# RWKV-7 in a two-layer hybrid block: a unit's two pairs prepared beside each other, and 32x32 triangles inverted as 16x16 blocks in the second layer

## The chip, the cores and the metric

One core of one Trainium2 chip. The metric is the time of one execution in device microseconds. Of the kernel before there are three: 2938.81, 2939.93 and 2939.21 us, median 2939.21 us.

## What is computed

A block of a latent diffusion generator, two layers deep, width 1024, in f32: 256 context tokens and 256 latent tokens, batch 1. Each layer normalizes and modulates the tokens, projects them with one wide matrix, and runs three mixers beside each other, each in both directions: mLSTM (4 heads), a depthwise convolution with an RG-LRU, and RWKV-7 (16 heads of 64). Sigmoid gates merge the three; an output projection, a residual and a SwiGLU follow. The last layer needs no context output. The mixer of this case is RWKV-7; the state of each head is 64x64, and a token does this:

```python
def step(s, x_t):
    r_t, w_t, k_t, v_t, kap_t, kapa_t = x_t
    s_kap = jnp.einsum('bhvk,bhk->bhv', s, kap_t)
    s = s * w_t[:, :, None, :] - s_kap[..., None] * kapa_t[:, :, None, :] + v_t[..., None] * k_t[:, :, None, :]
    return s, jnp.einsum('bhvk,bhk->bhv', s, r_t)
```

The kernel does it in chunks of 32 tokens. For each chunk, head and direction it needs the inverse of a unit triangular 32x32 matrix, built from products of `kap` and the keys.

## The kernel before

A layer is written in four parts. The first weaves the RWKV-7 work with the projections; the second runs the mLSTM heads and the RG-LRU, with the merge gates' projections beside them; the third merges and projects; the fourth is the SwiGLU. The weight blocks are f32, split by ScalarE (`whi`) and VectorE (`wlo`) into two parts, so that a block is 24 matmuls of 128x128 by up to 512 columns.

**Units.** RWKV-7 is done in eight units a layer: four groups of four heads (two pairs of two heads), each for 256 context tokens and then 256 latent tokens. A unit has 16 chunk-directions (8 chunks, 2 directions).
- `rw_load` reads the unit's r, k and v back from DRAM, once the rows of the unit before are done.
- `rw_prep` makes the decays and the rows, first for pair 0, then for pair 1 (`decay`, `rows`), and then the chunks' triangles (`chunks`, line 765): matmuls, a mask on VectorE into the tile `Am` (line 779), and four DMAs that write the strict triangles to DRAM, one matrix a partition row (line 786). Units are prepared one after the other.
- `rw_solve` (line 948) loads the 64 matrices of 32x32 as `N`, one on each of 64 partitions (line 955), inverts them on GpSimd with 30 pairs of a product and a subtraction (lines 961, 963), stores them (line 968) and loads them back into `Am` with four DMAs (line 973). All these go through SyncE's queue, which is in order.
- `rw_tok` transposes values and keys; `rw_chain` (line 977) walks the eight chunks, each needing the state that the one before left: matmuls into `xy`, `u` and `sc`, copies on VectorE and ScalarE between (lines 1032, 1059, 1062, 1079).
- `rw_tail` normalizes and gates the unit's output.

**Order.** `weave` decides at build time in which order the instructions of all these tasks and of the projections (`products`, the fill, last in the list) stand on each engine. It keeps a clock with costs given in the code; a task can yield a wait for a time, for another task's event, or for a lock on PSUM. The fill goes in when nothing else is ready, or first whenever less than `COLS[l]` columns of matmuls lie in the last `TICK` of its clock:

```python
light = [x for x in ready if x[3]]
if light:
    i = light[0]
elif fill in ready:

    if sum(c for _, c in recent) < cols + (HYS if burst else -HYS):
        i = fill
```

On the chip each engine runs its list in order. The gates' projections (`gemm`, line 423; loads on SyncE's queue, line 397; stores, line 1287) are not woven: the framework's scheduler places them after the projections, beside whatever follows. In layer 1 they and part of the projections have 256 columns, as only latent tokens are needed.

Of the kernel before, what the change touches and what calls it, by code (L numbers as in the profile page):

```python
# [11 lines left out]
F32 = mybir.dt.float32  # L12
F32R = mybir.dt.float32r
AF = mybir.ActivationFunctionType
ALU = mybir.AluOpType
# [19 lines left out]
COLS = [3000, 3000]  # L35
GDP = 1
ORD = [0, 0]
SL = 1000
# [61 lines left out]
def constants():  # L100
    c = {}
    c["ident"] = np.eye(128, dtype=np.float32)
    bo = np.zeros((128, 2), np.float32)
    bo[:64, 0] = 1
    bo[64:, 1] = 1
    c["bones"] = bo
    s = np.arange(32)[:, None]
    t = np.arange(32)[None, :]
    mk = np.zeros((2, 64, 64), np.float32)
    for d in range(2):  # L110
        st = (s < t).astype(np.float32)
        inc = ((s <= t) if d == 0 else (s <= 31 - t)).astype(np.float32)
        mk[d, :32, :32] = st
        mk[d, 32:, :32] = st
        mk[d, :32, 32:] = inc
        mk[d, 32:, 32:] = inc
    c["masks"] = np.concatenate([np.concatenate([mk[0], mk[0]], 0), np.concatenate([mk[1], mk[1]], 0)], 1)
    sm = np.ones((128, S), np.float32)
    sm[:, ::CH] = 0
    c["scanm"] = sm  # L120
    return c


CST = [("ident", 128), ("bones", 2), ("masks", 128), ("scanm", S)]
# [87 lines left out]
class KB:  # L212
# [349 lines left out]
    def rw_low(self, l, pss):  # L562
# [4 lines left out]
        for i, n in enumerate(("dd", "ad")):  # L567
            x, xd = (re.tile([128, T], F32, name=t, tag=t) for t in (("kap", "th"), ("bp", "ah"))[i])
# [91 lines left out]
    def rw_prep(self, l, u, ctx_out):  # L660
# [15 lines left out]
        Am = rl.tile([128, 2, 2, 8, 64], F32, name="Am", bufs=3)  # L676
# [22 lines left out]
        def wtanh(j, zw):  # L699
            p = 2 * q + j  # L700
            th = re.tile([128, 2, S], F32, name="th")
            for d in range(2):
                SC.activation(out=th[:, d], in_=zw[:, d], func=AF.Tanh, scale=0.5, bias=self.hdec[:, 8 * d + p:8 * d + p + 1])
                yield self.at("S", 470)
            return th

        def decay(j, th, za):
            p = 2 * q + j
            at = re.tile([128, 2, S], F32, name="at")
# [10 lines left out]
            pp = re.tile([128, 2, 8, 33], F32, name="pp")  # L720
# [7 lines left out]
            kt = re.tile([128, 2, S], F32, name="kt")  # L728
# [36 lines left out]
        def chunks(bks):  # L765


            for d in range(2):
# [14 lines left out]
            for j in range(2):  # L783
                for x in range(2):
                    b = 64 * x + 32 - 32 * j
                    nc.sync.dma_start(out=sc1[x, j].rearrange("q s t -> s q t"), in_=Am[b:b + 32, j, :, :, 0:32].rearrange("p d c t -> p (d c) t"))
# [6 lines left out]
        w = yield from axsplit(w)  # L793
        yield ("lock", "sm")
# [26 lines left out]
        sc1 = self.dr.tile([2, 2, 16, 32, 32], F32, name="sc1")  # L821
        bks = []
        for j in range(2):
# [5 lines left out]
            else:  # L829

                if u:
                    yield ("until", ("prep", l, u - 1))
                if yo:
                    bp = re.tile([128, 2, S], F32, name="bp")
# [3 lines left out]
            if j:  # L838
                th = yield from wtanh(1, zw)
            x = yield from decay(j, th, za)  # L840
            if not j:
                w = self.rw_aux(l, 2 * q + 1)
            bk = yield from rows(j, x)
            bks.append(bk)
            if j:
                self.done.add(("rows", l, u))
        yield from chunks(bks)
        yield ("spawn", self.rw_solve(l, u, Am, sc1))
        yield ("spawn", self.rw_tok(l, u, ctx_out, bks, bp, v, dict(kr=kr, Am=Am, PL=PL)))

    def rw_tok(self, l, u, ctx_out, bks, bp, v, unit):
# [12 lines left out]
        vr = self.tmp([128, 8, 2, 32], "kt")  # L864
# [83 lines left out]
    def rw_solve(self, l, u, Am, sc1):  # L948
# [907 lines left out]
```

## Time and profile before

| what | value |
|---|---|
| median of three runs | 2939.21 us |
| the profiled execution, its span | 2936.28 us, 2934.6 us |
| mean granted clock of TensorE, as a share of full speed | 0.965 |
| TensorE matmuls busy | 2648.2 us, 90% |
| VectorE, ScalarE busy | 1764.4 us (60%), 1266.3 us (43%) |
| GpSimd busy | 811.2 us, 28% |
| lines 961 and 963, GpSimd's inversions | 288.3 and 289.5 us |

Engines in the rows: PE is TensorE's matmuls, PEld its weight loads, DVE VectorE, ACT ScalarE, POOL GpSimd, SP SyncE; SPq is SyncE's queue, where a row is the issue of a DMA and not its transfer. The trace counts an f32 matmul of the program as two. A busy share is an average over parts with different limits, so the trace is cut into stretches: the woven part of layer 0 lies between some 110 and 830 us, its heads up to 1062; the woven part of layer 1 between 1711 and 2455 us, its heads up to 2613.

### The profile page before, as it was taken

How to read it: one execution, taken by the hardware profiler on the slowest of the kernel's cores; microseconds unless marked ns; L12 is line 12 of the kernel's file. 1: busy time of each engine (PE TensorE's matmuls, PEld its weight loads, DVE VectorE, ACT ScalarE, POOL GpSimd, SP SyncE). 2: the span in 40 equal slices, each digit the busy share in tenths (PEclk: the TensorE clock that was granted, in tenths of full speed). 3: DMA queues.
4: the chain of work that ended last, by engine and by line, in shares of the span. 5: the costliest groups of instructions: out<-in, count | busy, mean ns of one | idle time of the engine just before them, and what ended most of it. 6: DMA issues, size and time to landing. Idle time of an engine off the chain costs nothing. (4 is left out here: it accounts for less than half of the span.)

```text
span 2934.6 us, 70988 instructions
## 1 busy us (share of the span) xinstructions
PE 2648.2 (90%) x29512; PEld 2042.8 (70%) x29512; DVE 1764.4 (60%) x3642; ACT 1266.3 (43%) x2495; POOL 811.2 (28%) x1231
## 2 busy tenths in 40 slices
PE   7998889899999899999999999998988776769998
PEld 4876666666655576777777878776667655349898
DVE  5576767666478734553333466667676646867664
ACT  4444333343256632342222355444444323755553
POOL 1046555455212200010000100666556540100000
PEclk9999999999999999999999999999999787879999
DMA  6543333343354366655554445543344234237454
GB/s 222 179 137 108 101 107 105 106 113 92 109 198 138 104 230 224 220 171 171 166 166 137 124 148 167 152 122 112 117 121 124 77 106 157 83 96 257 147 185 139
DMA packets 242307, 421.04 MB, mean 143 GB/s; under 512 B 86048, under 2 KB 133408, under 8 KB 241984
## 3 DMA queue, kind: packets, MB, share of 16 engines
q1 hardware_dynamic: 219952, 339.89, 37.3%
q10 hardware_dynamic: 22032, 76.61, 8.4%
q8 instruction: 231, 3.78, 0.5%
q14 instruction: 92, 0.75, 0.1%
HBM read 348.75 MB, written 66.62 MB: 142 GB/s over the span
## 5 line engine op out<-in xcount | busy, mean ns | idle before, releaser
L258 PE MATMUL mm<-hl,whi 128*128 128x512 f32 (+1 forms) x1184 | 450.5, 380 | 4.8 <-DVE stage L547 4.0
L258 PE MATMUL mm<-hh,whi 128*128 128x512 f32 (+1 forms) x1184 | 450.6, 381 | 0.0
L258 PE MATMUL mm<-hh,wlo 128*128 128x512 f32 (+1 forms) x1184 | 449.8, 380 | 0.5 <-DVE wlo L471 0.5
L381 DVE TENSOR_TENSOR wlo<-wraw,whi 128x512 fp32r<-128x512 f32 (+1 forms) x310 | 214.7, 694 | 270.5 <-ACT whi L380 266.8
L423 PE MATMUL mm<-hl,whi 128*128 128x512 f32 (+1 forms) x1056 | 371.3, 352 | 2.8 <-ACT fg L1761 1.9
L423 PE MATMUL mm<-hh,wlo 128*128 128x512 f32 (+1 forms) x1056 | 364.6, 346 | 5.6 <-DVE wlo L381 5.6
L423 PE MATMUL mm<-hh,whi 128*128 128x512 f32 (+1 forms) x1056 | 366.3, 347 | 0.0
L380 ACT CAST whi<-wraw 128x512 fp32r<-128x512 f32 (+1 forms) x310 | 189.6, 614 | 371.2 <-PE mm L423 243.7
L961 POOL TENSOR_TENSOR et<-N 64x30 f32<-64x30 f32 (+14 forms) x480 | 288.3, 601 | 56.4 <-DMA N<-sc 20.1
L963 POOL TENSOR_TENSOR N<-N,et 64x30 f32<-64x30 f32 (+14 forms) x480 | 289.5, 603 | 37.4
L471 DVE TENSOR_TENSOR wlo<-wraw,whi 128x512 fp32r<-128x512 f32 x296 | 232.7, 787 | 104.4 <-ACT whi L468 100.0
L1205 POOL TENSOR_TENSOR nsq<-nsq,stage 128x256 f32<-128x256 f32 (+1 forms) x28 | 26.1, 932 | 879.3 <-ACT stage L1203 661.1
L258 PEld LDWEIGHTS mm<-hl,whi 128*128 128x128 f32 x1184 | 224.8, 190 | 49.1 <-issue 4.3
L258 PEld LDWEIGHTS mm<-hh,whi 128*128 128x128 f32 x1184 | 224.7, 190 | 42.8 <-issue 1.2
L258 PEld LDWEIGHTS mm<-hh,wlo 128*128 128x128 f32 x1184 | 224.6, 190 | 42.3 <-DVE wlo L471 1.7
L380 ACT CAST whi<-wx 128x512 fp32r<-128x512 f32 x212 | 128.7, 608 | 264.5 <-PE mm L423 164.7
L423 PEld LDWEIGHTS mm<-hl,whi 128*128 128x128 f32 x1056 | 203.1, 192 | 48.5 <-ACT whi L380 15.6
L381 DVE TENSOR_TENSOR wlo<-wx,whi 128x512 fp32r<-128x512 f32 x212 | 144.7, 683 | 147.8 <-ACT whi L380 141.7
L468 ACT CAST whi<-wraw 128x512 fp32r<-128x512 f32 x296 | 181.3, 617 | 113.9 <-PE mm L258 71.5
L423 PEld LDWEIGHTS mm<-hh,wlo 128*128 128x128 f32 x1056 | 203.3, 193 | 34.9 <-DVE wlo L381 6.4
L423 PEld LDWEIGHTS mm<-hh,whi 128*128 128x128 f32 x1056 | 203.3, 193 | 23.1 <-issue 1.5
L1519 PE MATMUL mm<-ylo,whi 128*128 128x256 f32 (+1 forms) x544 | 186.4, 343 | 19.5 <-DVE ylo L381 19.3
(321 smaller groups left out, 5284.2 us busy)
## 6 DMA issues: line engine op xcount, KB each, us to landing
wraw<-in_wA_dram ACTq DMA_DIRECT2D x144, 512.0 KB, 3.6
wraw<-in_wA_dram SPq DMA_DIRECT2D x131, 512.0 KB, 3.5
wx<-in_wA_dram SPq DMA_DIRECT2D x81, 512.0 KB, 3.5
wx<-in_wM_dram SPq DMA_DIRECT2D x55, 512.0 KB, 4.8
wraw<-in_wM_dram SPq DMA_DIRECT2D x41, 512.0 KB, 3.9
mld<-stage SPq DMA_DIRECT2D x48, 256.0 KB, 3.0
wraw<-in_wB_dram SPq DMA_DIRECT2D x23, 512.0 KB, 3.6
pd<-stage SPq DMA_DIRECT2D x40, 256.0 KB, 2.4
```

Of the source, the lines that this page charges most:

```text
L258: self.nc.tensor.matmul(out, lhsT, rhs, start=start, stop=stop)
L380: self.nc.scalar.copy(hi[i], x[i])
L381: self.nc.vector.tensor_tensor(out=lo[i], in0=x[i], in1=hi[i].bitcast(F32), op=ALU.subtract)
L423: self.nc.tensor.matmul(ps, x[k], y[:, koff + k, t0:t0 + n], start=start and i == 0, stop=stop and i == 3 * nk - 1)
L468: self.nc.scalar.copy(hi, x)
L471: self.nc.vector.tensor_tensor(out=lo, in0=x, in1=hi.bitcast(F32), op=ALU.subtract)
L961: G.tensor_tensor(out=tv, in0=N[:, 0:i, i:i + 1].broadcast_to([64, i, w]), in1=N[:, i:i + 1, i + 1:32].broadcast_to([64, i, w]), op=ALU.mult)
L963: G.tensor_tensor(out=N[:, 0:i, i + 1:32], in0=N[:, 0:i, i + 1:32], in1=tv, op=ALU.subtract)
L1205: (eng or self.nc.gpsimd).tensor_tensor(out=nsq, in0=nsq, in1=sq, op=ALU.add)
L1519: self.nc.tensor.matmul(ps, x[k], y[k][:, t0:t1], start=i == 0, stop=i == 3 * KC - 1)
```

## The change

- In both layers a unit's pair 1 is prepared by a task of its own, started from that of pair 0 (`pair`), and `chunks` becomes a task too, so the next unit's preparation starts at the event `rows`. Tiles `th`, `at`, `pp` and `kt` get two buffers.
- `Am` has two buffers instead of three and is taken in `chunks`, which first waits for the chain of two units before.
- In layer 1 (`BLOCKED`) a triangle of 32x32 is inverted as two 16x16 triangles, 128 matrices on 128 partitions, with 14 pairs on GpSimd; the off-diagonal block is the product of one inverse, the block and the other inverse, negated through the diagonal's sign: 64 matmuls into PSUM, one ScalarE read with a mask on odd halves (`Z`), 64 matmuls more, and four copies into `Am`. The inverses come back in eight DMAs into `Am` and four into `PT`, transposed.
- `COLS` of layer 1 goes from 3000 to 2400.

```diff
-COLS = [3000, 3000]
+COLS = [3000, 2400]
+BLOCKED = [0, 1]
...
-        Am = rl.tile([128, 2, 2, 8, 64], F32, name="Am", bufs=3)
...
-        def chunks(bks):
+        def chunks(bks, sc1):
+            if u > 1:
+                yield ("until", ("chain", l, u - 2))
+            Am = rl.tile([128, 2, 2, 8, 64], F32, name="Am", bufs=2)
...
             for j in range(2):
                 for x in range(2):
-                    b = 64 * x + 32 - 32 * j
-                    nc.sync.dma_start(out=sc1[x, j].rearrange("q s t -> s q t"), in_=Am[b:b + 32, j, :, :, 0:32].rearrange("p d c t -> p (d c) t"))
+                    for k in range(2 if BLOCKED[l] else 0):
+                        b = 64 * x + 32 - 32 * j + 16 * k
+                        nc.sync.dma_start(out=sc1[k, x, j].rearrange("q s t -> s q t"), in_=Am[b:b + 16, j, :, :, 16 * k:16 * k + 16].rearrange("p d c t -> p (d c) t"))
+                    if not BLOCKED[l]:
+                        b = 64 * x + 32 - 32 * j
+                        nc.sync.dma_start(out=sc1[x, j].rearrange("q s t -> s q t"), in_=Am[b:b + 32, j, :, :, 0:32].rearrange("p d c t -> p (d c) t"))
+            yield ("spawn", (self.rw_solve32, self.rw_solve16)[BLOCKED[l]](l, u, Am, sc1))
+            yield ("spawn", self.rw_tok(l, u, ctx_out, bks, bp, v, dict(kr=kr, Am=Am, PL=PL)))
...
         w = yield from axsplit(w)
+        w1 = self.rw_aux(l, 2 * q + 1)
...
-        sc1 = self.dr.tile([2, 2, 16, 32, 32], F32, name="sc1")
-        bks = []
-        for j in range(2):
+        sc1 = self.dr.tile([2, 2, 2, 16, 16, 16] if BLOCKED[l] else [2, 2, 16, 32, 32], F32, name="sc1")
+        bks = [None, None]
+
+        def pair(j, w, zw):
+
             if j:
                 w = yield from axsplit(w)
                 yield ("lock", "sm")
                 zw = low(w, self.low["dd"], 0)
                 yield self.took(SWL)
             else:
-
-                if u:
-                    yield ("until", ("prep", l, u - 1))
-                if yo:
-                    bp = re.tile([128, 2, S], F32, name="bp")
                 yield ("lock", "sm")
             za = low(w, self.low["ad"], 1)
             yield self.took(SWL)
             if j:
-                th = yield from wtanh(1, zw)
-            x = yield from decay(j, th, za)
-            if not j:
-                w = self.rw_aux(l, 2 * q + 1)
-            bk = yield from rows(j, x)
-            bks.append(bk)
-            if j:
-                self.done.add(("rows", l, u))
-        yield from chunks(bks)
-        yield ("spawn", self.rw_solve(l, u, Am, sc1))
-        yield ("spawn", self.rw_tok(l, u, ctx_out, bks, bp, v, dict(kr=kr, Am=Am, PL=PL)))
+                zw = yield from wtanh(1, zw)
+            else:
+                yield ("spawn", pair(1, w1, None))
+            x = yield from decay(j, zw, za)
+            bks[j] = yield from rows(j, x)
+            self.done.add(("pair", l, u, j))
+
+
+        if u:
+            yield ("until", ("prep", l, u - 1))
+        if yo:
+            bp = re.tile([128, 2, S], F32, name="bp")
+        yield from pair(0, w, th)
+        yield ("until", ("pair", l, u, 1))
+        self.done.add(("rows", l, u))
+        yield ("spawn", chunks(bks, sc1))
...
+    def rw_solve16(self, l, u, Am, sc1):
+        nc, V, G, SC, re = self.nc, self.nc.vector, self.nc.gpsimd, self.nc.scalar, self.re
+        if u:
+            yield ("until", ("solve", l, u - 1))
+        yield ("wait", DMW)
+        N = re.tile([128, 16, 16], F32, name="N")
+        nc.sync.dma_start(out=N, in_=sc1.rearrange("k x h q s t -> (k x h q) s t"))
+        yield ("wait", DML)
+        et = re.tile([128, 64], F32, name="et")
+        for i in range(1, 15):
+            w = 15 - i
+            tv = et[:, 0:i * w].rearrange("p (a b) -> p a b", b=w)
+            G.tensor_tensor(out=tv, in0=N[:, 0:i, i:i + 1].broadcast_to([128, i, w]), in1=N[:, i:i + 1, i + 1:16].broadcast_to([128, i, w]), op=ALU.mult)
+            yield ("on", self.op("G", 280 + 2.3 * i * w) - 1500)
+            G.tensor_tensor(out=N[:, 0:i, i + 1:16], in0=N[:, 0:i, i + 1:16], in1=tv, op=ALU.subtract)
+            yield ("on", self.op("G", 340 + 2.1 * i * w) - 1500)
+        G.memset(N.rearrange("p s t -> p (s t)")[:, 0:256:17], -1.0)
+        NT = re.tile([64, 16, 16], F32, name="NT")
+        G.tensor_copy(NT, N[0:64].rearrange("p s t -> p t s"))
+        yield ("on", self.op("G", 900) + LAT)
+        sc2 = self.dr.tile([3, 2, 2, 16, 16, 16], F32, name="sc2")
+        nc.sync.dma_start(out=sc2[0:2].rearrange("k x h q s t -> (k x h q) s t"), in_=N)
+        nc.sync.dma_start(out=sc2[2].rearrange("x h q s t -> (x h q) s t"), in_=NT)
+        yield ("wait", DML)
+        PT = re.tile([128, 16, 16], F32, name="PT")
+        HJ = [(x, j, 64 * x + 32 - 32 * j) for x in range(2) for j in range(2)]
+        for x, j, b in HJ:
+            nc.sync.dma_start(out=PT[b:b + 16], in_=sc2[2, x, j].rearrange("q s t -> s q t"))
+            for k in range(2):
+                r = slice(b + 16 * k, b + 16 * k + 16)
+                nc.sync.dma_start(out=Am[r, j, :, :, 16 * k:16 * k + 16].rearrange("p d c t -> p (d c) t"), in_=sc2[k, x, j].rearrange("q s t -> s q t"))
+        yield ("wait", DMR)
+        yield ("lock", "sm")
+        ps = self.sm([128, 16, 16])
+        for c in range(16):
+            for x, j, b in HJ:
+                self.mmul(ps[b:b + 32, c], Am[b:b + 16, j, c // 8, c % 8, 0:32], PT[b:b + 16, c])
+        yield self.took()
+        Z = re.tile([128, 16, 16], F32, name="Z")
+        SC.activation(out=Z, in_=ps, func=AF.Identity, scale=self.c["odd"])
+        yield self.end("S", 420)
+        ps = self.sm([128, 16, 16])
+        for c in range(16):
+            for x, j, b in HJ:
+                self.mmul(ps[b:b + 16, c], Z[b:b + 32, c], Am[b:b + 32, j, c // 8, c % 8, 16:32])
+        yield self.took()
+        for x, j, b in HJ:
+            o = Am[b:b + 16, j, :, :, 16:32]
+            p = ps[b:b + 16].rearrange("p (d c) t -> p d c t", d=2)
+            if j:
+                SC.copy(o, p)
+            else:
+                V.tensor_copy(o, p)
+            self.op("VS"[j], 420)
+        self.locks.discard("sm")
+        self.ready[u] = max(self.free[e] for e in "VS") + LAT
+        self.done.add(("solve", l, u))
+    def rw_solve32(self, l, u, Am, sc1):
...
```

Line numbers of the changed kernel are 2 higher from some line 230 on, and 74 higher behind the new function. SyncE's queue at the end of layer 1's woven part, before; `N` is the inverted triangles of unit 6, `wraw` a weight block, `mgd` the gates' store:

```order
L955 DMA N<-sc_25565 64x1024
L924 DMA ax<-in_aux_dram 128x512
L397 DMA wraw<-in_wA_dram 128x1024 x3
L1287 DMA mgd<-stage 128x256 x2
L397 DMA wraw<-in_wA_dram 128x1024
L968 DMA sc_26936<-N 64x1024
```

And with the change, the last unit's stores and first loads, and further on the first of the gates' weight blocks (`lrd` is a projection's store, `gt` and `ysc` belong to `rw_tail`):

```order
L984 DMA sc_27951<-N 128x256
L985 DMA sc_27951<-NT 64x256
L1353 DMA lrd<-stage 128x512
L990 DMA PT<-sc_27951 16x16x16
L993 DMA Am<-sc_27951 16x16x16 x2
```

```order
L1353 DMA lrd<-stage 128x512
L1201 DMA gt<-gate 128x2x256
L1353 DMA lrd<-stage 128x256
L399 DMA wraw<-in_wA_dram 128x1024 x2
L1684 DMA ysc_18345<-gt 128x2x256
```

The weight blocks of the gates stood between the stores of the inverted triangles; now they stand behind all of them.

TensorE where layer 1's chains end, before (`sc<-cst,Y` is the last unit's transpose, `mvT` the first head's):

```order
L423 MATMUL mm<-hl,whi 128x256
L423 MATMUL mm<-hh,whi 128x256
L423 MATMUL mm<-hh,wlo 128x256
L258 MATMUL sc<-cst,Y 64x2x32 x16
L1442 MATMUL sc<-cst,mvT 128x128 x4
```

And with the change, at the transpose, and at the first head:

```order
L260 MATMUL mm<-hh,wlo 128x512
L260 MATMUL mm<-hl,whi 128x512
L260 MATMUL mm<-hh,whi 128x512
L260 MATMUL sc<-cst,Y 64x2x32 x16
L260 MATMUL mm<-hh,wlo 128x512
```

```order
L425 MATMUL mm<-hl,whi 128x256
L425 MATMUL mm<-hh,whi 128x256
L425 MATMUL mm<-hh,wlo 128x256
L1516 MATMUL sc<-cst,mvT 128x128 x6
L1497 MATMUL sm<-cst,W_29101 128x36 x4
```

Before, all 576 gate products (line 423) stood ahead of the transpose; now 31 products of the projections (line 260) and 72 gate products (line 425) stand between it and the first head, and 504 gate products behind that.

## Rows read from the trace of the kernel before

**Rows 1.** Stretches: length, busy PE, PEld, DVE, ACT, POOL (counts), clock, DMA share, GB/s.
```profile
770.00:830.00 60.00, 58.31 (x901) 40.99 (x901) 33.03 (x102) 19.02 (x43) 1.76 (x4) 1.00 0.40 132
830.00:1022.00 192.00, 171.51 (x667) 100.90 (x666) 157.81 (x363) 130.24 (x232) 45.55 (x73) 0.98 0.42 137
...
1711.00:1860.00 149.00, 144.38 (x1131) 123.84 (x1130) 95.59 (x173) 78.93 (x150) 27.89 (x36) 0.99 0.54 168
1860.00:2290.00 430.00, 380.41 (x7236) 299.11 (x7234) 291.62 (x616) 193.82 (x431) 257.69 (x382) 0.98 0.42 121
2290.00:2455.00 165.00, 123.84 (x2427) 103.35 (x2421) 84.39 (x189) 50.09 (x120) 60.84 (x103) 0.83 0.34 96
2455.00:2613.00 158.00, 104.83 (x392) 56.55 (x391) 119.97 (x292) 97.93 (x177) 19.40 (x47) 0.78 0.34 107
```

**Rows 2.** Waits of TensorE from 2290 to 2700 us: in total, times, longest.
```profile
PE u L258 <- ACT UV L1059: 31.4, 10, 15.0
PE mm L1519 <- DVE ylo L381: 14.1, 4, 7.1
PE sc L1442 <- DMA mvT<-mld: 10.5, 1, 10.5
```

**Rows 3.** Timeline of SyncE's queue at the end of layer 1's woven part: start, time.
```profile
2288.79 0.33 SPq L397 DMA_DIRECT2D wraw<-in_wA_dram  x1
2312.07 0.45 SPq L968 DMA_DIRECT2D sc<-N  x1
2312.63 0.53 SPq L397 DMA_DIRECT2D wraw<-in_wA_dram  x1
...
2391.14 0.45 SPq L968 DMA_DIRECT2D sc<-N  x1
```

**Rows 4.** Timeline of TensorE at 2397 us, with the idle time before in brackets.
```profile
2397.02 0.70 PE L258 MATMUL u<-UV,bkT 64*64 64x64 f32 x16 [14.98 <-ACT UV L1059]
```

**Rows 5.** Groups of GpSimd: the page's, then layer 1's by shape.
```profile
L961 POOL TENSOR_TENSOR et<-N 64x30 f32<-64x30 f32 (+14 forms) x480 | 288.3, 601 | 56.4 <-DMA N<-sc 20.1
...
L963 POOL TENSOR_TENSOR N<-N,et 64x58 f32<-64x58 f32 x16 | 5.9, 368 | 1.3
...
L961 POOL TENSOR_TENSOR et<-N 64x30 f32<-64x30 f32 x16 | 4.4, 278 | 14.3 <-DMA N<-sc 13.6
```

**Rows 6.** Timeline of TensorE between 2336 and 2348 us: start, time.
```profile
2336.84 0.28 PE L423 MATMUL mm<-hh,whi 128*128 128x256 f32 x1
2336.97 0.28 PE L423 MATMUL mm<-hh,wlo 128*128 128x256 f32 x1
...
2343.39 1.25 PE L258 MATMUL sm<-cst,v 64*32 64x64 f32 x64
...
2347.08 0.26 PE L258 MATMUL u<-xs,Am 32*32 32x64 f32 x4 [1.06 <-DVE xs L1032]
...
2347.30 0.27 PE L258 MATMUL xy<-UV,Am 32*32 32x64 f32 x5
```

**Rows 7.** Timeline of SyncE's queue for units of layer 1: Am out, Am back.
```profile
2036.63 4.85 SPq L786 DMA_DIRECT2D sc<-Am  x4
...
2109.58 3.48 SPq L973 DMA_DIRECT2D Am<-sc  x4
```

**Rows 8.** Timeline of VectorE: the first step of the chain of that unit.
```profile
2115.38 0.29 DVE L1032 COPY xs<-xy 128x128 f32<-128x128 f32 x1 [1.33 <-PE xy L258]
```

**Rows 9.** TensorE's busy time of line 423 alone, 2245 to 2455 us: first, sum.
```profile
2245.00:2290.00 45.00, 16.70 (x108) 0.99 0.49 127
...
sum 210.00, PE 99.13; mean PE 19.83
```

**Rows 10.** Sums of stretches, 1837 to 2272 us: six inversions, then what lies between.
```profile
sum 263.00, PE 231.36 PEld 177.28 DVE 197.00 ACT 117.22 POOL 228.39; mean PE 38.56 PEld 29.55 DVE 32.83 ACT 19.54 POOL 38.06
...
sum 172.00, PE 157.12 PEld 130.03 DVE 97.31 ACT 79.22 POOL 33.84; mean PE 26.19 PEld 21.67 DVE 16.22 ACT 13.20 POOL 5.64
```

**Rows 11.** The page's group of VectorE's subtraction that splits weights.
```profile
L381 DVE TENSOR_TENSOR wlo<-wraw,whi 128x512 fp32r<-128x512 f32 (+1 forms) x310 | 214.7, 694 | 270.5 <-ACT whi L380 266.8
```

More of the change, by code (lines that the diff above doesn't have):

```diff
@@ L116, in constants @@
         mk[d, 32:, 32:] = inc
+    c["odd"] = (np.arange(128) % 32 >= 16).astype(np.float32)[:, None]
     c["masks"] = np.concatenate([np.concatenate([mk[0], mk[0]], 0), np.concatenate([mk[1], mk[1]], 0)], 1)
@@ L121, in constants @@
     return c
-CST = [("ident", 128), ("bones", 2), ("masks", 128), ("scanm", S)]
+CST = [("ident", 128), ("bones", 2), ("masks", 128), ("scanm", S), ("odd", 1)]
 COFF = {}
@@ L567, in rw_low @@
         for i, n in enumerate(("dd", "ad")):
-            x, xd = (re.tile([128, T], F32, name=t, tag=t) for t in (("kap", "th"), ("bp", "ah"))[i])
+            x, xd = (re.tile([128, T], F32, name=t, tag=t, bufs=2 if t == "th" else 1) for t in (("kap", "th"), ("bp", "ah"))[i])
             yield from self.shifted(pss[i], 24 + i, 2, x)
@@ L700, in wtanh @@
             p = 2 * q + j
-            th = re.tile([128, 2, S], F32, name="th")
+            th = re.tile([128, 2, S], F32, name="th", bufs=2)
             for d in range(2):
@@ L708, in decay @@
             p = 2 * q + j
-            at = re.tile([128, 2, S], F32, name="at")
+            at = re.tile([128, 2, S], F32, name="at", bufs=2)
             for d in range(2):
@@ L719, in decay @@
             yield self.at("V", 910)
-            pp = re.tile([128, 2, 8, 33], F32, name="pp")
+            pp = re.tile([128, 2, 8, 33], F32, name="pp", bufs=2)
             V.memset(pp[:, 0, :, 0:1], 1.0)
@@ L727, in decay @@
             self.op("S", 633)
-            kt = re.tile([128, 2, S], F32, name="kt")
+            kt = re.tile([128, 2, S], F32, name="kt", bufs=2)
             SC.activation(out=kt, in_=at, func=AF.Identity, scale=self.hka[:, p:p + 1], bias=self.omka[:, p:p + 1])
@@ L863, in rw_tok @@
             t = self.op("G", 1904, self.free["V"])
-        vr = self.tmp([128, 8, 2, 32], "kt")
+        vr = self.tmp([128, 8, 2, 32], "kt", 2)
         SC.copy(vr[:, ::-1, :, ::-1].rearrange("p c j t -> p j c t"), v.rearrange("p j (c t) -> p j c t", t=CH))
@@ L946, in rw_load @@
             self.done.add(("load", l, u))
-    def rw_solve(self, l, u, Am, sc1):
+    def rw_solve16(self, l, u, Am, sc1):
[55 more added lines that the diff above has]
+        self.done.add(("solve", l, u))
```

## The prediction

> **What bounds the kernel now.** The span of the profile is 2934.6 us; the profiled execution took 2936.3 us, and the median of the three runs is 2939.2, 2.9 above it, so 2.9 is added at the end. I read the stretches first, because the change touches two of them and the share of busy time is an average over all. Each layer has a woven part, where projections and the RWKV-7 units share TensorE, and behind it a part with the mLSTM heads and the RG-LRU (the heads, below). In layer 1 the reader is to see four rows [rows 1]: TensorE is busy 144.4 of 149 us, then 380.4 of 430, then only 123.8 of 165 at a granted clock of 0.83, then 104.8 of 158 at 0.78. So TensorE bounds the woven part until about 2290 us, and from there to 2613 us it is starved. The last chains outlive the projections: from 2245 us on, gate products of line 423 are the fill [rows 9], and by 2455 they are used up, so nothing is left for the heads.
>
> The waits of TensorE name the cause [rows 2]: 31.4 us before matmuls into `u`, two of them about 15 us long. ScalarE stands there as releaser, but the DMA queue tells more [rows 3]: SyncE issues a weight load at 2288.8 us, then nothing until 2312.1, when it stores N, and the next weight load goes out 0.6 us later. The store waits for GpSimd's inversion, and the weights of the gates stand behind it. At 2391.1 us the same happens, and TensorE goes on at 2397.0 after 15.0 us [rows 4]. Line 961 takes 288.3 us over 16 inversions [rows 5], 18 each; line 963 works on the same shapes and takes as much; with the gaps between the 60 instructions an inversion takes some 42 us.
>
> **What the change does to the work.** *Inversion, layer 1.* 60 GpSimd instructions of up to 240 elements become 28 of 14 to 56. The nearest forms take 0.278 us at 30 elements and 0.368 at 58 [rows 5]: 28 x 0.31 = 9 us, 2 us of gaps, 1 us for the diagonal and the transposed copy, so 12 us in place of 42. The 30 us a unit are off TensorE's path by themselves; what they bring is that nothing waits behind them.
>
> *Block product.* 1024 matmuls are added, which the trace counts as 2048, since each f32 matmul there is two. From above: 64 small ones issue in 1.10 us, 17 ns each (1.25 with the last one's tail) [rows 6], so 2048 x 17 = 35 us. From below: in four positions of 32x32, 30 of them start within 0.22 us [rows 6], 7.5 ns each, so 15 us. I take 15 and 3 us for the starts of 16 groups, 18 in all, because the products use the same four positions. The Trainium skill, TensorEngine Tiling (Array Packing), section Performance Considerations (Instruction Overhead), speaks against this edit: a matmul of one column takes as long as one of 60, and one should not tile a dimension that is already small. By it the 16 columns save nothing over the 64 of the rows, which the 7.5 ns already allow for; with the upper row the sum would be 17 us more. ScalarE and VectorE get one read of PSUM and two to four small ones a unit; both have idle time in every stretch [rows 1], and I put them at nothing.
>
> *SyncE queue.* A unit issues 8 stores of Am instead of 4, 2 stores and 12 loads instead of 1 and 4: 13 more. Four Am loads took 3.5 us of the queue and four stores 4.9 [rows 7], so 0.9 to 1.2 us each where it is crowded, 11 to 16 us more a unit, on a queue with some 65 us a unit. Stores of projections stand behind them. The order shows no weight load there any more: the projections' own go through ScalarE's queue, and the gates' come after the last chain.
>
> *Pairs beside each other, and Am in two buffers.* The next unit's preparation starts when the rows of this one exist, not after its triangles. But the triangles now wait for the chain of two units before, since Am has two buffers. For that loop I take one unit [rows 7, 8]: from the stores of Am at 2036.6 us to the first step of its chain at 2115.4 there are 79 us. Less 30 on GpSimd, plus 11 to 16 on SyncE, makes 60 to 65 at worst, and some 45 with half of the queue's delays gone. TensorE's own work between the two is a unit's pitch less the triangles, 56 us (from 65 and 9). So in the likely case it doesn't wait there. I allow 1.5 us a unit, 12 in all, for this and for the read of PSUM between the two products.
>
> *Order.* `COLS` falls from 3000 to 2400 in layer 1: projections go ahead of other work only while fewer columns than that lie in the planner's window, so fewer of them stand between the chains' steps and more are left over. In layer 1 the projections end after the last chain, where before they ended three chains sooner. All 576 gate products move behind the chains: 72 ahead of the heads, 195 among them, 309 behind. In layer 0 the same shift moves 163 gate products from the chains; 181 stand among the heads and 395 behind, where it was 223 and 190.
>
> **The sum.** *Layer 1.* TensorE's busy time from 1711 to 2455 us is 648.6 us [rows 1]. The gates hold 99.1 of it [rows 9], and other work at the lower clock some 5 too much: 544 remain. With the product it is 562. TensorE's idle share in the inversions' stretches is 12.0% (31.6 of 263), between them 8.7% (14.9 of 172) [rows 10]. I take the higher, as there is less fill for each chain: 562/0.88 is 639, plus 12 makes 651, and the projections end at 1711 + 651 = 2362 us, with the last chain just ahead. The heads took 158 us before [rows 1], with 10.5 us of waiting for a load [rows 2], in which the 72 gates now fit. The 195 gates are 8 blocks or 16 halves, each a VectorE subtraction of 0.694 us [rows 11]; half of these 11 us fall into idle time, so the heads take 164 and end at 2526. The 309 others take 0.12 us each [rows 6], 37 us; 2563. The merge began at 2613 before: 50 us less. It then waited 14.1 us for `ylo` [rows 2], whose loads the 309 gates now cover; I count 10 of these. Layer 1: 60 us less.
>
> *Layer 0.* TensorE is busy 58.3 us from 770 to 830 [rows 1], of which the 163 gates at 512 columns, twice 0.12 us each, are 39. Without them the heads start near 790 instead of 830. They take 187 instead of 192 (42 gates fewer, of which VectorE, busy 157.8 of the 192, lets half count), to 977, and 395 dense gates add 95: 1072 against 1062. So 9 us more, with -1 to +14 as its ends. GpSimd and the chain keep their cost here.
>
> 2936.3 - 60 + 9 = 2885 us, and 2888 as a median.
>
> **The rivals.** *More is gained.* GpSimd's load on VectorE may be what makes TensorE idle: VectorE is busy 75% within inversions and 57% between [rows 10]. If the idle share falls to 8.7% and the added 12 us don't come, the woven part takes 616 us, not 651: 2853 us. Against it: the products, too, wait on chains, and preparation is denser. The Trainium skill, GPSIMD Engine Reference, section 1 (Specifications), says that GpSimd shares its SBUF interfaces with VectorE instructions that have two inputs there; these two rows agree with that, without showing how much of the difference it makes. Chance 0.14.
>
> *The gates are no good fill.* Between the heads TensorE stood at 0.78 of its clock [rows 1]. If that stays, 267 gates run at the lower of the two levels, 1.2 GHz, 0.09 us more each: 25 us, 2913. Against it: layer 0's heads, with gates among them, ran at 0.98. Chance 0.16.
>
> *TensorE waits for the block product: slower.* The place is the first product of each unit: TensorE runs in order, so all behind it stands while the twelve loads and what they wait for are late. If the loop takes 65 us, its worst case above, the wait is 9 us a unit, not 1.5, 60 us in all: 2948. It decides from 8 us a unit (52 us of gain over 8 units, and the 1.5). For it: 13 more issues in one queue, and the Am wait makes each chain depend on the one two before. Against it: no matmul of a chain waits for its Am load now, with the inversion 30 us longer. Chance 0.11.
>
> *No effect.* If TensorE were fully fed in the tail, a shorter inversion would change nothing: 2939. The 31.4 us of waits [rows 2] speak against it. Chance 0.04.
>
> **How the numbers follow.** The forecast has the remaining 0.55, with 2862 to 2913 as its own range, from the product (18 against 35), the layer-0 ends and 12% against 10 to 14% of idle time. 2845 to 2935 takes in both faster rivals; left out are the slower one, no effect, and a few in a hundred below. Faster by over 0.2% (6 us, about what a measurement of this kernel can tell) is 0.85, within it 0.04, slower 0.11.
>
> **What would show it.** Right: GpSimd some 200 us less busy in the woven part of layer 1; no wait of 15 us at `u`; the projections ending near 2362 us, just behind the last chain; a clock over 0.9 among the heads; 95 us of dense gates ahead of layer 0's merge. Wrong: TensorE waiting at the first product for a DMA in each unit, a pitch between units that stays at 70 us, or heads of over 190 us in layer 1.

## The result, and the profile after

The changed kernel takes 2898.62 us (median of four runs, 2894.72 to 2907.76), the kernel before 2939.57 (four runs): ratio 0.9859, 95% interval 0.9842 to 0.9876, so 41 us faster. A second series gave 2895.06 us (five runs, 2887.44 to 2896.22; ratio 0.9857, 0.9831 to 0.9882). The profiled execution below is the longest of its four, 2907.76 us; that of the second series took 2887.44 with the same instructions, and both are used where they differ.

The page of the changed kernel: busy time by engine, and a queue of instructions (packets, MB, share of 16 DMA engines).

```profile
PE 2686.3 (92%) x31560; PEld 2071.4 (71%) x31560; DVE 1730.7 (60%) x3658; ACT 1273.0 (44%) x2520; POOL 606.4 (21%) x983
...
q8 instruction: 248, 4.06, 0.6%
```

GpSimd is busy 205 us less. The stretches of the changed kernel, columns as in [rows 1]: layer 0's heads and the dense gates behind them, then layer 1's woven part, heads and dense gates.

```profile
792.00:968.00 176.00, 154.44 (x578) 87.43 (x576) 139.75 (x331) 119.93 (x217) 39.58 (x70) 0.95 0.40 130
968.00:1074.00 106.00, 100.62 (x426) 80.91 (x425) 42.58 (x64) 39.14 (x67) 5.07 (x3) 0.97 0.55 182
1724.00:2384.00 660.00, 600.76 (x12287) 474.19 (x12287) 401.05 (x949) 295.10 (x651) 134.64 (x271) 0.94 0.40 113
2384.00:2548.00 164.00, 135.56 (x626) 87.07 (x625) 127.91 (x306) 109.77 (x207) 21.52 (x47) 0.88 0.45 136
2548.00:2598.00 50.00, 42.60 (x311) 40.27 (x309) 28.91 (x47) 28.45 (x56) 2.06 (x2) 0.90 0.73 220
```

Before, layer 1 went from 1711 to its merge at 2614 us, 903 us; now from 1724 to 2598, 874 (870 in the second profile). The stretch in which TensorE was busy 123.8 of 165 us [rows 1] is gone: TensorE is busy 91% until the projections end. But the granted clock there is 0.94, where before it was 0.98 and more until 2290 us. The second row starts before layer 0's last head ends, at 975 us; behind it stand 395 gate products, until 1074 us.

What TensorE waits for in the changed kernel (what waits, releaser: us in total, times, the longest), from 1724 to 2384 us; with the next group it answers to [rows 2]:

```profile
PE sm L260 <- DMA Am<-sc: 15.7, 13, 3.6
PE sm L260 <- issue: 9.1, 10, 1.7
PE u L260 <- ACT UV L1133: 8.9, 17, 1.5
```

From 2384 to 2700 us, with the heads, the dense gates and the merge:

```profile
PE mm L425 <- DVE wlo L383: 13.6, 7, 4.3
```

No wait of the chains at `u` is longer than 1.5 us, where two were some 15 [rows 2, 4]. New are the waits of the block product for its loads. The waits at `sm` for nothing that the profile shows ("issue") are not all new: the kernel before has 7.1 us of them from 1712 to 2384 us, and of the 9.1 here 6.3 stand before the product.

The chains now follow each other closely. In the changed kernel's timeline (start, length in us, engine, line; in brackets the idle time before) the last copy into `UV` of layer 1's third unit is:

```profile
2069.01 0.26 ACT L1133 COPY UV<-u 32x128 f32<-32x128 f32 x1 [0.36 <-DVE UV L1136]
```

and the first copy into `xs` of the fourth, 5.3 us after its end, where before 16.1 us passed until 2115.38 us [rows 8]:

```profile
2074.53 0.28 DVE L1106 COPY xs<-xy 128x128 f32<-128x128 f32 x1
```

The seven gaps between a layer's eight chains, worked out the same way and added up, and where its last chain ends, all in us:

| kernel | layer 0: gaps, end | layer 1: gaps, end |
|---|---|---|
| before | 139.8, 807 | 112.7, 2447 |
| changed | 76.7, 762 | 39.0, 2368 |
| old inversion in both layers | 76.8, 756 | 64.8, 2425 |
| pairs one after the other | 139.8, 804 | 140.9, 2414 |
| block inversion in both layers | 60.4, 733 | 37.6, 2356 |

### The profile page after: what moved, and what is told of

It is laid out like the page before. It is cut to its first block, busy times and chain, and to the rows that moved or that the text cites. A ratio compares the mean times of both kernels' runs of the same rounds, so it can differ in the third digit from the quotient of the medians.

```text
span 2906.0 us, 75026 instructions
## 1 busy us (share of the span) xinstructions
PE 2686.3 (92%) x31560; PEld 2071.4 (71%) x31560; DVE 1730.7 (60%) x3658; ACT 1273.0 (44%) x2520; POOL 606.4 (21%) x983
## 3 DMA queue, kind: packets, MB, share of 16 engines
q8 instruction: 248, 4.06, 0.6%
## 5 line engine op out<-in xcount | busy, mean ns | idle before, releaser
L473 DVE TENSOR_TENSOR wlo<-wraw,whi 128x512 fp32r<-128x512 f32 x296 | 224.9, 761 | 109.1 <-ACT whi L470 107.9
L1133 ACT COPY UV<-u 32x128 f32<-32x128 f32 x256 | 65.4, 255 | 294.5 <-DVE UV L1136 293.5
L1593 PE MATMUL mm<-yhi,wlo 128*128 128x256 f32 (+1 forms) x544 | 179.8, 331 | 0.9 <-DVE wlo L383 0.9
```

What stands on the lines that cost most here:

```text
L473: self.nc.vector.tensor_tensor(out=lo, in0=x, in1=hi.bitcast(F32), op=ALU.subtract)
L1133: SC.copy(UV[j][b, :, i], us[b, j])
L1593: self.nc.tensor.matmul(ps, x[k], y[k][:, t0:t1], start=i == 0, stop=i == 3 * KC - 1)
```

## The experiments

Twelve series, eleven of variants and one of the changed kernel again, each with runs of the kernel before on the same chip beside it; ratios are to these. Gains and costs below are differences of medians. Theory: the time comes from layer 1's tail, where the stalls at SyncE's queue end and gates are kept for the heads. Rivals: the preparation gives it; `COLS` gives or takes it; the block product eats it.

### Each part undone

```diff
-COLS = [3000, 2400]
+COLS = [3000, 3000]
```

> The changed kernel with COLS of layer 1 back at 3000. Theory A (2400 is part of the gain: it keeps projections in stock for the last chains and leaves the gates for the heads): the projections end two chains before the last chain ends (near 2300 us in place of 2384), gate products of line 425 fill the last chains, fewer are left for the heads, which run at a clock near 0.8; about 2915 us, 15 to 20 slower than the changed kernel. Rival B (2400 is what lowers the clock in the woven part, 0.94 there against 0.98 before): the clock among the chains returns to 0.97 or more and the time falls to about 2885 us. If it is within 5 us of 2898.6, the number decides nothing here.

2889.32 us, ratio 0.9839 (0.9813 to 0.9865). Neither theory: projections ended at 2364 us, the last chain at 2355, no gate stood among the chains, and the woven part's clock was 0.95, against 0.94 in the changed kernel.

```profile
1714.00:2364.00 650.00, 599.56 (x12269) 469.56 (x12269) 395.49 (x942) 292.08 (x650) 132.00 (x269) 0.95 0.40 113
```

This part took 650 us, against 660 and 661 in the changed kernel; but with the block inversion in both layers (below) it took 665 with 3000 and 656 with 2400. `COLS` moves nothing that can be measured. The gates stand behind the chains because the chains end sooner.

```diff
-BLOCKED = [0, 1]
+BLOCKED = [0, 0]
```

> The changed kernel with the old inversion of whole 32x32 triangles in layer 1 too; pairs beside each other, Am in two buffers and COLS 2400 stay. Theory A (the short inversion is the gain; with the long one the wait of the triangles for the chain of two units before sets the pitch, as in layer 0, where from the end of a chain to the start of the one two later there are 76 to 82 us): pitch of 70 us or more in layer 1, the projections end before the last chain, 15 to 30 us slower than the changed kernel, 2915 to 2930 us. Rival B (the block product, its waits for loads and the low clock behind it cost as much as the shorter inversion gives): within 6 us of 2898.6, with the clock in the woven part at 0.97 or more.

2927.53 us, ratio 0.9962 (0.9946 to 0.9978): theory A. The projections ended at 2320 us, the last chain at 2425, and a wait of 15.9 us at `u` is back, as is that of the merge for `ylo`. In its waits from 2230 to 2720 us:

```profile
PE u L260 <- ACT UV L1133: 22.2, 15, 15.9
PE mm L1593 <- DVE ylo L383: 13.4, 4, 7.1
```

The pairs alone (`COLS` with them) are worth 12 us.

```diff
-        yield ("spawn", chunks(bks, sc1))
+        yield from chunks(bks)
...
-            Am = rl.tile([128, 2, 2, 8, 64], F32, name="Am", bufs=2)
+        Am = rl.tile([128, 2, 2, 8, 64], F32, name="Am", bufs=3)
...
-        yield from pair(0, w, th)
+        for j in range(2):
```

> The kernel before with the block inversion and COLS 2400 in layer 1: the pairs of a unit are prepared one after the other as before, Am has three buffers and the triangles do not wait for a chain. Theory A (all of the gain is in the inversion and the order of layer 1, and the pairs beside each other cost some 10 us in layer 0, where the merge began at 1074 us in place of 1062): layer 0 as before, layer 1 as in the changed kernel or a little later, 2885 to 2900 us. Rival B (the preparation closes the gaps between the chains, 13 to 26 us before and 4 to 10 after): the gaps in layer 1 stay over 10 us, the pitch at 70 us, and the time is 2915 to 2930 us.

2920.0 us, ratio 0.9934 (0.9912 to 0.9956): rival B. The chains themselves are short, 406 us for eight against 460 in the changed kernel, but the gaps between them are 140.9 us, since the next unit is not prepared. The block inversion alone is worth 19 us. 12 and 19 make 31; together they give 41, some 10 more, which is hardly more than three such series leave uncertain (their intervals are 5 to 7 us to either side).

```diff
-BLOCKED = [0, 1]
+BLOCKED = [1, 1]
```

> The changed kernel with the block inversion in layer 0 too. Theory A (in layer 0 TensorE is busy 93% of the woven part with projections to spare, so a shorter inversion frees nothing there, and 18 us of product, waits for its loads and a lower clock behind each product are added): 10 to 25 us slower than the changed kernel, 2908 to 2924 us, layer 0's heads starting 10 to 25 us later than 792 us. Rival B (the wait of the triangles for the chain of two units before sets the pitch of 70 us in layer 0, and 30 us less of inversion shortens it): pitch of 65 us or less in layer 0, 10 to 20 us faster, 2879 to 2889 us.

2889.10 us, ratio 0.9841 (0.9815 to 0.9867), the changed kernel's time within the intervals, so neither theory. In layer 0 the pitch stayed at 70 us (chains from 209 to 699 us in seven steps); the last chain ends 16 to 29 us sooner, at 733 us, and yet the projections end later, at 798, and the merge begins at 1069, between the 1062 and 1074 of the two profiles of the changed kernel. TensorE bounds this stretch (busy 650.3 of 688 us):

```profile
110.00:798.00 688.00, 650.28 (x13131) 482.93 (x13131) 433.76 (x1060) 282.75 (x610) 132.38 (x279) 0.97 0.37 114
```

The shorter inversion and the added product together changed nothing there that could be measured; what the one gave and the other cost isn't separated.

### The changed kernel again, and its product

> The changed kernel itself, beside the next three, on one chip. Its four runs gave 2894.7 to 2907.8 us, and its first layer, the same code as in the variant with COLS 3000, ended 8 us later there. Theory A (the order is the same, and the granted clock sets the difference: COLS 2400 and the block inversion in layer 0 change nothing): 2885 to 2898 us here. Rival B (both variants are really faster than it, by 9 us): 2895 us or more.

2895.06 us, as given above, inside both theories' ranges: nothing tells the two variants of about 2889 us from it. For both variants together:

```diff
-COLS = [3000, 2400]
+COLS = [3000, 3000]
-BLOCKED = [0, 1]
+BLOCKED = [1, 1]
```

> The changed kernel with COLS 3000 and the block inversion in both layers. Theory A (neither matters, TensorE bounds both woven parts): the time of the changed kernel within 6 us. Rival B (each gave 9 us and they add): 2880 us, or 15 to 20 us faster than the changed kernel.

2897.48 us, ratio 0.9873 (0.9851 to 0.9896): theory A; the two do not add.

```diff
-        for c in range(16):
+        for c in [c for _ in range(2) for c in range(16)]:
```

(in both halves of the product)

> The changed kernel with each of the 1024 matmuls of the block product issued twice into the same place. Theory A (a product of 64 matmuls takes 1.2 us, 9.4 ns a record, as in its first clean occurrences, and nothing else hangs on it): 16 times 1.2, some 20 us slower than the changed kernel. Rival B (the low activity of the product makes the clock fall behind it, so that it costs more than its own time): 30 us or more slower, with the woven part of layer 1 at a clock lower than 0.94. Rival C (it lies in idle time): less than 8 us.

2955.80 us, ratio 1.0067 (1.0047 to 1.0088): 61 us slower than the changed kernel, twice what rival B asked for. The two halves of the product from 1716 to 2430 us (us busy, mean ns of one, us idle before them and its releasers):

```profile
L260 PE MATMUL sm<-PT,Am 16*32 16x16 f32 x2048 | 26.1, 190 | 32.3 <-issue 24.1 <-DMA Am<-sc 8.2
L260 PE MATMUL sm<-Am,Z 32*16 32x16 f32 x2048 | 20.0, 186 | 21.1 <-issue 21.1
```

One product of it on the timeline, columns as above:

```profile
2212.33 1.85 PE L260 MATMUL sm<-PT,Am 16*32 16x16 f32 x201 [0.34 <-DMA Am<-sc]
2217.84 0.76 PEld L260 LDWEIGHTS sm<-PT,Am 16*32 16x32 f32 x49 [3.76 <-issue]
...
2221.07 1.86 PE L260 MATMUL sm<-Am,Z 32*16 32x16 f32 x202
2225.33 0.50 PEld L260 LDWEIGHTS sm<-Am,Z 32*16 32x16 f32 x54 [2.51 <-issue]
```

After some 200 matmul records and as many weight loads TensorE stands for 2 to 4 us with nothing named as releaser (what ends these gaps is worked out in the last section). The clock in this stretch is 0.91:

```profile
1716.00:2430.00 714.00, 626.80 (x14295) 497.42 (x14294) 395.82 (x942) 293.86 (x649) 129.81 (x269) 0.91 0.34 104
```

Next, the product left out, and with it the read of PSUM and the copies into `Am` (`rw_solve16` ends after its loads):

```diff
-        yield ("wait", DMR)
...
-        for c in range(16):
-            for x, j, b in HJ:
-                self.mmul(ps[b:b + 32, c], Am[b:b + 16, j, c // 8, c % 8, 0:32], PT[b:b + 16, c])
...
+        self.ready[u] = max(self.now, self.since) + DMR
```

> The changed kernel without the block product in layer 1: its 1024 matmuls, the read of PSUM and the copies into Am are left out, the loads stay, so the inverses miss their off-diagonal block. Theory A (the product costs its own 18 to 27 us and no more): 15 to 30 us faster than the changed kernel (2895). Rival B (with the gaps without a releaser, the waits for loads and the low clock behind it, it costs what doubling it added, some 60 us): 45 to 65 us faster. Rival C (what it takes lies in time in which TensorE would wait for a chain anyway): less than 10 us.

2848.96 us, ratio 0.9715 (0.9693 to 0.9738): the product costs 46 us, rival B at its lower end. By the ratios to the kernel before it is 42, known to some 10 us. Without it the woven part, to the last chain's end, runs at a clock of 0.98:

```profile
1717.00:2333.00 616.00, 571.89 (x10263) 452.96 (x10262) 389.57 (x925) 287.23 (x633) 130.34 (x267) 0.98 0.40 123
```

In the changed kernel the two halves hold 26.5 us of TensorE, and 22.1 of idle time stand before them, from 1724 to 2384 us:

```profile
L260 PE MATMUL sm<-PT,Am 16*32 16x16 f32 x1024 | 15.4, 196 | 15.7 <-DMA Am<-sc 15.7
...
L260 PE MATMUL sm<-Am,Z 32*16 32x16 f32 x1024 | 11.1, 186 | 6.4 <-issue 6.3
```

How the cost divides can be read from layer 1's start to its merge, with the product and without it:

```profile
1724.00:2598.00 874.00, 778.92 (x13220) 601.53 (x13219) 557.86 (x1301) 433.32 (x911) 158.22 (x320) 0.92 0.43 123
1717.00:2537.50 820.50, 740.87 (x11168) 573.68 (x11166) 545.59 (x1277) 420.28 (x881) 155.62 (x320) 0.95 0.42 130
```

Of the 53.5 us between them 26.5 are the product's own, 11.5 are longer busy time of the same other work, and 15.5 are more idle time. With the second profile of the changed kernel, 870 us, they are 27, 6 and 16.

The lower clock is not the product's alone. With the pairs one after the other the product is there too, and the clock is 0.97 until the projections end; with the old inversion and the new preparation there is no product, and it is 0.96:

```profile
1706.00:2294.00 588.00, 543.03 (x10079) 431.59 (x10078) 347.73 (x814) 272.13 (x591) 114.53 (x234) 0.97 0.42 122
1716.00:2320.00 604.00, 531.61 (x8520) 420.64 (x8518) 411.50 (x819) 271.03 (x581) 306.76 (x451) 0.96 0.39 124
```

The next two move the waits and the order around the product.

```diff
-        yield ("wait", DMR)
+        yield ("wait", DMR + 4000)
```

> The changed kernel with the planner's wait between the twelve loads and the first product raised from 5 to 9 us, so that other work stands ahead of the product in TensorE's order. Theory A (TensorE's waits for these loads, 16 us in 11 to 13 waits, and the low clock behind them are on the path): the waits at the product fall to a few us, the clock in the woven part rises by 0.01 or more, 10 to 20 us faster than the changed kernel. Rival B (the chains follow each other without a gap and the product's end releases the next one: what TensorE gains, the chain loses): within 6 us.

2891.03 us, ratio 0.9841 (0.9818 to 0.9864): the time of rival B. The waits for the loads fell from 15.7 us to 0.9, those without a releaser rose from 9.1 to 15.8 at `sm` and from 14 to 24 at all tiles, the clock stayed at 0.94. Much of what the loads no longer held up, these gaps did:

```profile
PE sm L260 <- issue: 15.8, 16, 1.8
...
PE sm L260 <- DMA Am<-sc: 0.9, 2, 0.7
```

```diff
-        yield self.took()
+            if c % 4 == 3:
+                yield self.took()
+                yield ("wait", 0.0)
```

(in both halves of the product)

> The changed kernel with the block product in pieces of 16 matmuls, between which the planner may put projections or other work. In the variant with each matmul issued twice the time rose by some 60 us, 20 of it in the matmuls and 38 in gaps of 1 to 5 us with no releaser in the middle of the row of small matmuls. Theory A (a dense row of small matmuls outruns the delivery of TensorE's instructions and lets the clock fall; both cost time): the gaps without a releaser at the product (9 us in 10) go, the clock in the woven part rises, 8 to 20 us faster than the changed kernel (2895). Rival B (the chain waits for the whole product, which now takes longer): 0 to 15 us slower, the start of a chain more than 10 us after the end of the one before. Rival C: within 6 us.

2893.33 us, ratio 0.9846 (0.9823 to 0.9869): rival C. Nearly all of the product now stands in pieces of 32 records with other work between. The gaps between the chains stayed at 3 to 8 us, the idle time before the product's matmuls fell from 22.1 to 13.7 us while their busy time rose from 26.5 to 31.6, and the time did not move. Neither the loads' lateness nor the dense row is by itself what the product costs.

### The heads, and the queue

```diff
-MG = [[0, 0], [0, 0]]
+MG = [[0, 0], [2, 2]]
```

> The changed kernel with the gates of layer 1 placed by hand, two blocks ahead of and two behind each mLSTM head, so that all of the fill stands among the heads and little behind them; the computation is the same. In the changed kernel 268 to 292 of 576 gate matmuls stand among the heads, which take 150 us at a busy share of 83% and a clock of 0.88, and some 300 stand behind. Theory A (the heads are bound by VectorE and by their own waits, so what is put among them costs nearly what it costs behind): within 6 us of 2895. Rival B (the gates were no good fill because too few stand there): 10 to 20 us faster, the clock among the heads over 0.95. Rival C (in-order engines: the splits of the gates' weights on VectorE and ScalarE hold up the heads): 5 us or more slower.

2894.51 us, ratio 0.9852 (0.9829 to 0.9876): theory A. 410 gate matmuls stand ahead of and among the heads, in place of 267, and 166 behind, in place of 309; the heads take 162 us from their first matmul to their last, in place of 150 to 155. What one part gains the other loses.

```diff
-        nc.sync.dma_start(out=sc2.rearrange("x h q s t -> (x h q) s t"), in_=N)
+        nc.gpsimd.dma_start(out=sc2.rearrange("x h q s t -> (x h q) s t"), in_=N)
...
-                nc.sync.dma_start(out=Am[b:b + 32, j, :, :, 0:32].rearrange("p d c t -> p (d c) t"), in_=sc2[hd, j].rearrange("q s t -> s q t"))
+                nc.gpsimd.dma_start(out=Am[b:b + 32, j, :, :, 0:32].rearrange("p d c t -> p (d c) t"), in_=sc2[hd, j].rearrange("q s t -> s q t"))
```

> The kernel before with the store of the inverses and the four loads back into Am issued from GpSimd's queue in place of SyncE's, nothing else. Theory A (SyncE stood at the store until the inversion was done, and the gates' weights behind it starved TensorE): the two waits of 15 us at the matmuls into u go, 20 to 30 us faster than before (2936 to 2939), if the issue from GpSimd doesn't lengthen the loop. Rival B (the chain itself waits for the inversion, and the weights were no more than late in company): the waits stay, as waits of the chain's own matmuls, and the time is within 6 us of before.

2936.35 us, ratio 0.9994 (0.9979 to 1.0010): no gain, and part of both theories. The wait at 2297 us is gone (none over 1.5 us from 2280 to 2330), but at 2400 us a chain waits for its own inverses:

```profile
PE u L258 <- DMA Am<-sc: 14.0, 2, 12.6
```

From layer 1's start to its merge it takes 887 us against 903, and layer 0 gives 12 back: its merge begins at 1074 us in place of 1062. In layer 1 the last unit's inversion ended at 2404.0 us, and TensorE went on at 2410.5. So the queue held up the first wait and the inversion itself the second.

Three buffers of `Am` with the new preparation, which would take the wait for the chain of two units before away, were not tried; what that wait costs stays open.

## Why the prediction was right, and where it was not

Forecast 2888 us, 2845 to 2935, and 0.85 for faster; it came to 2898.6. 10 us of the gain are missing, and two terms were wrong by far more and against each other: the woven part's busy time came out 39 us longer and its idle time 30 us shorter.

| step | forecast, us | profile of the changed kernel, us |
|---|---|---|
| one inversion, with diagonal and transposed copy | 12 (before 42) | 11.8 to 12.9, eight of them |
| stores of `Am` to the chain's first step | some 45, at worst 65 (before 79) | 44 to 64, eight of them |
| SyncE's queue, more a unit | 11 to 16 | some 6 (12, before 4 to 8) |
| block product | 18, at most 35 | 42 to 46, by leaving it out |
| TensorE's idle time, layer 1 woven | 77 and 12 allowed | 59.2 (660 - 600.8) |
| its busy time there | 562 | 600.8 |
| length of that part | 651 | 660 (661 in the second profile) |
| heads, dense gates | 164, 37 | 164, 50 |
| merge shorter by | 10 | 13 (94 against 107) |
| layer 0's merge begins | 1072 (before 1062) | 1074 (1062 in the second) |

**Right.** The inversion's term and where it went: GpSimd is busy 212 us less among layer 1's chains, and no wait of 15 us is left. The heads of layer 1 and the order in layer 0 came as worked out: heads from 792 to 975 us, forecast 790 to 977, and behind them 99 us for 395 dense gates, forecast 95. The rival of a slower kernel at its place, the loads of the product, did come, in six of eight units, with 15.7 us in all, 2 a unit where 8 were needed; and taking these waits away brought nothing that could be measured, as raising the planner's wait showed.

**The step that failed most is the block product's 18 us.** It was priced from a burst of 30 records at 7.5 ns each [rows 6]. A record of its own costs 12.9 ns (26.5 us by 2048), and that is little over half of the 46. Beyond 12 us allowed for waits the sum had no term for what a row of small matmuls does around it: TensorE stands before and within it, and the clock of the woven part is 0.94, against 0.98 without it and 0.91 with it doubled. Each of the 2048 records also comes with a weight load, 4096 records in all, which take 16 packets of the instruction queue; no two of these start less than 3.2 us apart in any profile here (last section). The rule of the Trainium skill, TensorEngine Tiling (Array Packing), section Performance Considerations (Instruction Overhead), not to tile a dimension that is already small, pointed the right way; by the row that went with it the sum was 17 us more, 35, and even that falls short.

**The pairs were priced at an allowed wait and no gain.** Serial preparation costs 25 us (2920 against 2895). A chain needs its preparation and its inverses; each alone was late. With the old inversion every second gap in layer 1 is some 16 us, with the old preparation they are 8 to 33, and with both new they are 3 to 10.

**The rest of the busy time was taken at 544 us, and the idle share at 12%.** The woven part without the product's records holds 574.3 us (600.8 - 26.5). The 544 took the gates' 99.1 us and 5 more off the sum, but part of the gates' time overlaps with other matmuls. These are the matmuls of the helper's line alone (258, then 260), nearly all of this part but the gates: before, in the changed kernel with the product, and with the product left out (length, busy time and count of TensorE, clock, DMA share, GB/s):

```profile
1711.00:2456.00 745.00, 556.82 (x10200) 0.95 0.43 125
1724.00:2394.00 670.00, 597.39 (x12248) 0.94 0.41 115
1717.00:2357.00 640.00, 559.30 (x10200) 0.97 0.41 126
```

So 13 of the 30 us were there before (556.8 less 544), and most of the others come with the product. The idle share was 9.0%: 12% was that of the inversions' stretches alone [rows 10], and until its projections ended, at 2245 us, the kernel before had 8.5% (45 of 534 us).

**The order was put down to `COLS`**, which moves nothing that can be measured here; nearly the same order came with 3000. And **the stalls were put down to SyncE's queue**: true for one of the two.

**The dense gates** were taken at 0.12 us each; 309 hold 42.4 us, 0.137, at a clock of 0.90, and some 7 us of waits lie between, most for `wlo`. The clock among the heads is 0.88, not over 0.9. The account of the profile is then: layer 1 began 13 us later than before, not 9, the woven part took 9 us more than forecast, the dense gates 13 more, the merge 3 less; 2885 and 23 are its 2907.8. The median lies 9 us below.

## What to carry to other kernels

A step that needs two things is sped up little by making one of them early: the gaps ahead of layer 1's chains are 64.8 and 140.9 us with one of the two parts and 39.0 with both. Time these gaps with each part undone. Price a block of small matmuls by leaving it out or doubling it, not by its records: here it cost 42 to 46 us where its records held 26.5. And a stage in which TensorE is busy over 90% with work to spare, as layer 0's, need not gain from shorter chains: with the pairs beside each other its last chain ended 45 to 58 us sooner (762 and 749 us against 807), and its merge began at 1074 and 1062 us, against 1062.

## What was not expected of the hardware

A dense row of small matmuls met a limit that no semaphore shows. TensorE's 63,120 records and the 4.06 MB in 248 packets of the instruction queue make 64 bytes a record and some 255 records a packet; the trace gives each packet 16,384 bytes, which is 256 such records. With the product doubled there are 4096 records and 16 packets more:

```profile
q8 instruction: 264, 4.33, 0.6%
```

The gaps without a releaser at `sm` come after some 400 records within 2 us, and grew from 9.1 us to 47.3 in all. The packed trace has the time of every packet, and it shows what ends them. From 1700 to 2450 us the doubled kernel has 29 gaps without a releaser, at all tiles. 27 of them, 49.9 of 51.1 us, end at the same place in the count of 256 records, and 1.2 to 1.6 us after a packet has landed, whether the gap is 0.2 or 4.6 us long. The first one shown above ends at 2217.84 us, 1.44 us after a packet that landed at 2216.40; the second at 2225.34, 1.27 after one at 2224.06. In the changed kernel it is so for all 14, and in the kernel before for 7 of 8. TensorE waits there for its instructions. In none of the 14 profiles do two packets of this queue start less than 3.2 us apart, while a row passes 400 records in 1.9 us. By that spacing 16 packets more are an estimated 51 us where nothing lies ready; doubling the product took 61, 37 of them in such gaps (51.1 against 14). Why the packets come no closer no run shows.

In the changed kernel itself these gaps are not what the product costs: without it there are 12.7 us of them up to 2384 us, and 14 with it. What it brings there is the 15.7 us of waits for its loads; with these gone the gaps rose to 24 us, as shown above.

The Trainium skill, Perfetto Trace Analysis, section Per-instruction lifecycle (The 4-stage abstract model), gives 64 bytes for an instruction, and the trace agrees.

The same instructions took 670 us in layer 0's woven part in one profile of the changed kernel (110 to 780 us, clock 0.99) and 682 in the other (110 to 792, clock 0.97). And layer 1, the same code in the changed kernel and with the block inversion in both layers, took 870 and 874 us to its merge in the one and 864 in the other. Variants that differ by less than some 8 us can't be told apart here with five runs each (half of an interval of 0.9831 to 0.9882 is 7.5 us of 2936).
